# Loading FFN weight blocks a pair earlier in a hybrid decoder block, and packing float16 operands two to a buffer

## The chip, the cores and the metric

The kernel runs on one core of a Trainium2 chip. The metric is the device time of one execution in microseconds (us), lower is better. Engines are named as in the profile: PE (matrix multiply, PEld its weight loads), DVE (vector), ACT (scalar), POOL (gpsimd), SP (the queue that issues most DMAs).

## The reference

One block of a decoder on 1024 tokens of width 1024, float32. Two token mixers run side by side (dilated attention, and a gated causal convolution), they are gated and added, projected (`w_mix_out`), normalised and added to the input. A normalised SwiGLU feed-forward layer (FFN) follows:

```python
x = x + rms_norm(merged @ w_mix_out[l], g_post_mix[l])
h = rms_norm(x, g_pre_ffn[l])
x = x + rms_norm(swiglu_ffn(h, w_ffn_in[l], w_ffn_out[l]), g_post_ffn[l])

def swiglu_ffn(h, w_ffn_in, w_ffn_out):
    gate, up = jnp.split(h @ w_ffn_in, 2, axis=-1)
    return (jax.nn.silu(gate) * up) @ w_ffn_out
```

The hidden width is 2816, so `w_ffn_in` makes 22 gate blocks and 22 up blocks of 128 columns.

## The kernel before

**Precision.** Every product is made of split operands: an operand is written as a rounded part `hi` (ACT copies it) and a rest `lo` (DVE subtracts), and a product is `hi*hi + hi*lo + lo*hi`, three matmuls. In the FFN the parts are float16, and a weight block is first scaled by a power of two found from the block itself. That takes two steps. `peaks` (line 128, ACT) squares the block and sums the squares, and writes a bfloat16 column `pb` (L133 for a block, L131 for a pair). `scales` multiplies `pb` with a matrix of ones on PE (L140), which sums over the partitions, and DVE makes the scale of it (L143 to L147). Only then come the splits (L241 on ACT, L242 on DVE).

**Order by ticks.** The order on each engine is the order in which the program is written out, and each engine works strictly in that order. `tick()` is called after every few matmuls; in a tick come, in this order, the steps planned for it, one *piece* from the queue `pieces` (in each tick whose number divides by `PIECE`), and one step of each running background generator. So a piece or a planned step lands between two matmuls in PE's order, and between the work of two ticks in the order of ACT and DVE.

**Weights.** `jobs` lists all weight blocks in the order of use. `weights(i)` issues the DMA loads (L217, on SP) up to two jobs past `i`, queues the pieces of the jobs up to one past `i`, and returns the parts of block `i`; `ahead` (1 in the mixing projection) is added to both distances. A float32 block lives in a buffer of tag `b` (42 buffers of 4 KB a partition), a first block of a pair in tag `d` (3 buffers, "ring"). A plain FFN block has four pieces: `peaks`, `scales`, and a split of each half.

**Mixing projection** (L1659). Tiles of 128 tokens: first tiles 0 and 1 together, then tiles 2 to 7 one by one, each over eight blocks of `w_mix_out`. A tile has eight times six matmuls; after each six come two ticks, so a tile from 2 on has 16 ticks. `PIECE` is 2 in the first group and 3 after it. The weights of block 7 are asked for at the last of the eight blocks of the first group. After each tile a generator `mix_norm` starts: tick 1 squares (ACT L1344), tick 2 the root (L1331), ticks 3 and 4 DVE L1351, ticks 5 and 6 the addition of x (DVE L1355), tick 7 a store, tick 9 squares, root and scaled copy (ACT L1366, L1331, L1368). After tiles 3 and 7 there follow, from tick 18 on and every two ticks, four transposes on PE (L1376), a scaled copy out of them (ACT L1382) and a float16 split (L1242, L1243). PE writes `scales` and transposes into the same two PSUM banks in turn.

**FFN in.** The first two gate and two up blocks are multiplied plainly with the first and then with the second half of the tokens (`unit`: 24 matmuls, eight ticks, L368 to L372). The other 20 gate/up pairs go through `winograd`: seven products of 12 matmuls and four ticks (L384 to L386), 28 ticks a pair. Its products come in the order A11, A12, S2, S1, S3, S4, A22; S1 to S4 are sums of quarters of the two blocks. After A11 ACT copies a bank (L398), after S2 (L403; S3 goes on adding in that bank), after S1 (L408). After A12 follows DVE L1818, after S3 L1823 (A22 goes on adding in that bank), after S4 L1827. `quarters(i, c)` makes the operands of a pair in six steps: c=0 splits the first block, c=1 adds S1 and S2 (DVE L269, L270), c=2 splits them, c=3 adds S3 and S4 (L276, L277), c=4 splits them, c=5 splits A22. Steps 3 to 5 of the running pair and 0 to 2 of the next are put on ticks of the running pair by `pair`:

```python
todo = [(1, quarters(i, 3)), (8, quarters(i, 4)), (10, quarters(i, 5))]      # shortened
todo += [(LD, load_ahead(n + 1))]                                            # LD = 2
todo += [(PK, peaks(n + 1)), (SC, scales(n + 1))]                            # PK = 9, SC = 16
todo += [(k, quarters(n + 1, c)) for c, k in enumerate(PS)]                  # PS = (19, 17, 25)
```

**FFN out** (L1932) follows with its own loads and splits. `split` (L1242, L1243) makes a pair of parts in one buffer of tag `b`; for float16 it fills half of that buffer. It is used for the 16 tiles of the normalised activations (float16), the 16 activation sums T1 to T4 of the FFN (float16), and elsewhere for float32 parts.

Of the kernel before, what the change touches and what calls it, by code (L numbers as in the profile page):

```python
# [11 lines left out]
F16 = mybir.dt.float16  # L12
# [6 lines left out]
T = 1024  # L19
D = 1024  # L20
KT = 8
# [16 lines left out]

LD, PC = 2, (18, 20, 26)

PK, SC, PS = 9, 16, (19, 17, 25)

TINY, W_TOP, H_TOP = 2.0 ** -60, 2.0 ** -13, 128.0

# [21 lines left out]
def f(ap):  # L66
    return ap if ap.dtype == F16 else ap.bitcast(F32)


class Build:  # L70
# [117 lines left out]
    T, sums = None, None  # L188
# [139 lines left out]
    def timed(self, now, then, load, split):  # L328

        self.load_ahead(now[-1])  # L330
        self.queue_split(now[-1])
        self.flush(now[-1])
        self.plan.setdefault(self.ticks + load, []).append(lambda: self.load_ahead(then[-1]))
        self.plan.setdefault(self.ticks + split, []).append(lambda: self.queue_split(then[-1]))
        return [self.hl.pop(i) for i in now]

    def pair(self, i):


        J = self.jobs  # L340
        self.load_ahead(i)
        self.queue_split(i)
        self.flush(i)
        n, t = i + 1, self.ticks
        todo = [(1, lambda: self.quarters(i, 3)), (8, lambda: self.quarters(i, 4)), (10, lambda: self.quarters(i, 5))]
        if n < len(J) and J[n][2] == "row1":
            todo += [(LD, lambda: self.load_ahead(n + 1))]
            if n >= self.scaled:
                todo += [(PK, lambda: self.peaks(n + 1)), (SC, lambda: self.scales(n + 1))]
            todo += [(k, lambda c=c: self.quarters(n + 1, c)) for c, k in enumerate(PS if n >= self.scaled else PC)]  # L350
            if self.conv_sums:
                todo.append((22, self.channel_sum))
            self.queued = n + 2
        elif n < len(J):
            todo += [(3, lambda: self.load_ahead(n + 1)), (16, lambda: self.queue_split(n + 1))]
        for k, s in todo:
            self.plan.setdefault(t + k, []).append(s)
        return self.hl[i]
# [871 lines left out]
    def out_parts(self):  # L1230

        for hp in range(2):
# [3 lines left out]
            self.OT[hp] = self.both(x)  # L1236
            x = None

    def split(self, src, n, dt=F32R):
        nc = self.nc  # L1240
        s = self.slot(dt)
        nc.scalar.copy(s[:, :n], src)  # L1242
        nc.vector.tensor_tensor(s[:, 512:512 + n], src, f(s[:, :n]), op=OP.subtract)  # L1243
        return s
# [171 lines left out]
def build(ctx, tc, aps):  # L1416
    B = Build(ctx, tc, aps)
# [14 lines left out]
    glu_jobs = [(job(w_in[NG + j]), job(w_in[NU + j])) for j in range(FIRST)]  # L1432
    early = [job(w_in[NGC + n]) for n in range(8 - EARLY, 8)]
    glu_pairs = [pair(NG + j, NU + j) for j in range(FIRST, 8)]
    ga = [pair(NGA + n, NGA + n + 1) for n in range(0, 8, 2)]
    gc = [pair(NGC + n, NGC + n + 1) for n in range(0, 8 - LATE - EARLY, 2)]
    qkj = {(g, hp): pair(NK + 4 * g + hp, NQ + 4 * g + hp) for g in range(3) for hp in range(4)}
    vj = {(g, hg): (job(aps["w_v"][2 * g + hg, 0]), job(aps["w_v"][2 * g + hg, 1], kind="second"))
# [141 lines left out]
    for n, hf in [(0, 0), (1, 0), (0, 1), (1, 1)] + [(n, hf) for n in range(2, 8) for hf in range(2)]:  # L1580
# [11 lines left out]
        c = mg[n][:, hf * H:(hf + 1) * H]  # L1592
# [3 lines left out]
        if hf:  # L1596
            B.later(9, lambda n=n: nc.sync.dma_start(B.d_gc[n], mg.pop(n)))
            c = None
# [15 lines left out]
    for n in range(8):  # L1614
# [4 lines left out]
        for hf in range(2):  # L1619
            s = slice(hf * H, (hf + 1) * H)  # L1620
# [3 lines left out]
            x = B.slot(F32R)  # L1624
# [14 lines left out]
    def load_x(tt):  # L1639
        x = (B.half(), B.half())  # L1640
        for nh in range(2):
            nc.sync.dma_start(x[nh], aps["x"][tt * 128:(tt + 1) * 128, nh * H:(nh + 1) * H])
        return x
# [3 lines left out]
    for tiles in ((0, 1), (2,), (3,), (4,), (5,), (6,), (7,)):  # L1647
        banks = {tt: (B.bank(), B.bank()) for tt in tiles}
        for kt in range(KT):
            if len(W) == kt:  # L1650
                B.ahead = 1
                W.append(B.weights(mx[kt]))
            for tt in tiles:
                m = mop[tt // 4]
                o = (tt % 4) * 128
                for st, wt, a, b in ((m[kt][:, o:o + 128], W[kt][0], 1, 0), (m[kt][:, o:o + 128], W[kt][1], 0, 0),
                                     (m[kt][:, H + o:H + o + 128], W[kt][0], 0, 1)):
                    for nh in range(2):
                        nc.tensor.matmul(banks[tt][nh], st, wt[:, nh * H:(nh + 1) * H], start=bool(kt == 0 and a),  # L1659
                                         stop=bool(kt == KT - 1 and b))  # L1660
                B.tick()
                B.tick()
            if tiles[0] == 7:
                W[kt] = None
        B.PIECE = 3
        m = None
        for tt in tiles:
            if tt % 4 == 3:
                mop[tt // 4] = None
            if tt < 6:  # L1670
                xt[tt + 2] = load_x(tt + 2)
            for e in norms[:-1]:
                B.finish(e)
            norms.append(B.bg(B.mix_norm(tt, banks[tt], xt.pop(tt))))
# [2 lines left out]


    B.PIECE = 2
    held = {}  # L1680

    def spill(p, name, x):
# [129 lines left out]
    for j in range(PLAIN, FT):  # L1812
        s = [None, None]
# [108 lines left out]
    for i in range(7):  # L1922
# [12 lines left out]
        n = NP - LAST if i == 6 else NP  # L1935
        for p in range(n):
            k = i * NP + p
# [19 lines left out]
        elif i == 5:  # L1957
            for t in range(4):
                x2_load(4 + t)
                c = C[1][t][:, R]  # L1960
# [3 lines left out]
    for t in range(4):  # L1964
        for p in range(NP - LAST, NP):
            k = 6 * NP + p
# [82 lines left out]
```

## Time and profile before

| | |
|---|---|
| median of 3 runs | 1726.68 us (1723.57 to 1729.7) |
| the profiled execution, its own time | 1729.81 us |
| its span in the profile | 1728.0 us |
| PE busy | 1692.5 us (98%) |
| DVE / ACT / POOL busy | 1256.7 / 860.4 / 495.8 us |
| mean granted PE clock | 0.993 |
| mixing projection | about 991 to 1085 us of the span |
| FFN in, plain blocks | about 1085 to 1139 us |
| FFN in, 20 pairs | about 1139 to 1512 us |
| FFN out | about 1512 to 1722 us |

Times in rows are microseconds from the span's start. A row of the timeline gives start, duration, engine, line, operation, what it writes and reads, how many were merged, and in brackets how long the engine had been idle before it and which instruction ended that. A row of waits gives the total, the number and the longest. A row of windows gives the length of the stretch, the busy time and number of instructions of PE, PEld, DVE, ACT and POOL, the granted PE clock, the busy share of the DMA engines and GB/s. A matmul of 512 columns is listed with 0.38 us, but matmuls overlap, and the next starts about 0.22 us later.

### The profile page before, as it was taken

The numbers are of one execution on the slowest core, as the hardware profiler recorded it, in microseconds if no ns is written. First come the engines' busy times: TensorE is split into PE (matmuls) and PEld (weight loads), VectorE is DVE, ScalarE is ACT, GpSimd is POOL, SyncE is SP. The second block draws the span as 40 slices with busy tenths as digits, with TensorE's granted clock in tenths as the row PEclk, the third lists the DMA queues.
The fourth block names the chain that finished last, engine by engine and source line by source line (L and its number), as shares of the span: only waits on it lengthen the run. The fifth ranks groups of instructions, "written<-read, shape, count | busy, mean of one in ns | idle before, by whom it ended". The sixth has DMA issues, their size and how long they took to land.

```text
span 1728.0 us, 24733 instructions
## 1 busy us (share of the span) xinstructions
PE 1692.5 (98%) x8722; PEld 1289.3 (75%) x8722; DVE 1256.7 (73%) x2323; ACT 860.4 (50%) x1664; POOL 495.8 (29%) x386
## 2 busy tenths in 40 slices
PE   8999999999999999999999999899999999999998
PEld 7788888888888999999888887444444444488886
DVE  6789978889998656687664865586666666677586
ACT  6344343344444566667622356755445445454463
POOL 0017778887885245545300120000000000000000
PEclk9999999999999999999999999999999999999999
DMA  4352434445578697787935732212232232395244
GB/s 164 106 179 86 159 116 140 158 171 183 166 189 214 211 285 197 224 227 209 292 143 187 266 126 90 88 73 92 93 141 96 92 126 94 134 366 156 88 145 152
DMA packets 159626, 277.58 MB, mean 161 GB/s; under 512 B 47010, under 2 KB 78429, under 8 KB 159501
## 3 DMA queue, kind: packets, MB, share of 16 engines
q1 hardware_dynamic: 155292, 263.82, 47.2%
q0 software_dynamic: 3920, 11.91, 2.1%
q8 instruction: 69, 1.13, 0.3%
q14 instruction: 57, 0.46, 0.1%
q10 hardware_dynamic: 288, 0.27, 0.0%
HBM read 185.34 MB, written 95.33 MB: 162 GB/s over the span
## 4 chain that ended last, share of the span: by engine, by line
PE 82%; DMA 5%; DVE 5%; ACT 5%; issue 2%; POOL 1%; SPq 0%; DVEq 0%; ACTq 0%; POOLq 0%
PE p L384 13%; PE p L385 13%; PE p L386 13%; PE p L1932 12%; PE p L368 4%; PE p L372 4%; PE p L370 4%; PE p L1659 3%; DMA b<-w_fi 2%; PE p L1005 2%; PE p L1007 2%; PE p L1003 2%; PE p L617 2%; PE p L1101 2%; PE p L1137 1%
## 5 line engine op out<-in xcount | busy, mean ns | idle before, releaser
L384 PE MATMUL p<-b,b 128*128 128x512 f32 (+1 forms) x1124 | 432.6, 385 | 7.8 <-ACT c L403 7.8
L385 PE MATMUL p<-b,b 128*128 128x512 f32 (+1 forms) x1124 | 432.4, 385 | 0.0
L386 PE MATMUL p<-b,b 128*128 128x512 f32 (+1 forms) x1124 | 432.4, 385 | 0.0
L1932 PE MATMUL p<-b,b 128*128 128x512 f32 x924 | 209.8, 389 | 0.0
L1932 PEld LDWEIGHTS p<-b,b 128*128 128x128 f32 x924 | 173.4, 188 | 36.1
L747 DVE SCALAR_TENSOR_TENSOR p<-b,par,p 128x511 f32<-128x511 f32 (+14 forms) x232 | 163.9, 741 | 0.0
L368 PE MATMUL p<-b,b 128*128 128x512 f32 (+1 forms) x368 | 148.0, 402 | 0.0
L370 PE MATMUL p<-b,b 128*128 128x512 f32 (+1 forms) x368 | 147.1, 400 | 0.0
L372 PE MATMUL p<-b,b 128*128 128x512 f32 (+1 forms) x368 | 146.9, 399 | 0.0
L384 PEld LDWEIGHTS p<-b,b 128*128 128x128 f32 x644 | 120.9, 188 | 26.3 <-ACT c L403 0.7
L386 PEld LDWEIGHTS p<-b,b 128*128 128x128 f32 x644 | 120.9, 188 | 25.1
L385 PEld LDWEIGHTS p<-b,b 128*128 128x128 f32 x644 | 120.9, 188 | 24.9
L251 POOL TENSOR_TENSOR b<-d,b 128x1024 fp32r<-128x1024 f32 x44 | 106.9, 2429 | 79.9 <-ACT b L250 72.4
L1003 PE MATMUL p<-b,b 128*128 128x256 f32 x384 | 116.0, 302 | 0.0
L1005 PE MATMUL p<-b,b 128*128 128x256 f32 x384 | 115.2, 300 | 0.0
L1007 PE MATMUL p<-b,b 128*128 128x256 f32 x384 | 115.1, 300 | 0.0
L1242 ACT CAST b<-b 128x512 fp32r<-128x512 f32 (+1 forms) x117 | 72.2, 619 | 46.6 <-PE p L1932 18.0
L1243 DVE TENSOR_TENSOR b<-c,b 128x512 fp32r<-128x512 f32 (+1 forms) x101 | 70.4, 698 | 33.2 <-ACT b L1242 32.9
L385 PEld LDWEIGHTS <-b 128*128 128x128 f16 x480 | 46.9, 98 | 62.6 <-issue 8.2
L1243 DVE TENSOR_TENSOR b<-b,b 128x512 fp32r<-128x512 f32 (+1 forms) x117 | 80.1, 689 | 17.9 <-ACT b L1242 16.1
L1659 PE MATMUL p<-b,b 128*128 128x512 f32 x384 | 89.7, 392 | 0.0
L384 PEld LDWEIGHTS <-b 128*128 128x128 f16 x480 | 47.0, 98 | 56.9 <-issue 0.4
(273 smaller groups left out, 3530.4 us busy)
## 6 DMA issues: line engine op xcount, KB each, us to landing
b<-w_in SPq DMA_DIRECT2D x30, 512.0 KB, 4.7
dk<-c SPq DMA_DIRECT2D x48, 256.0 KB, 2.8
dq<-c SPq DMA_DIRECT2D x48, 256.0 KB, 3.7
b<-dq SPq DMA_DIRECT2D x48, 256.0 KB, 8.6
b<-dk SPq DMA_DIRECT2D x48, 256.0 KB, 7.0
b<-w_fi SPq DMA_DIRECT2D x24, 512.0 KB, 4.8
d<-w_in SPq DMA_DIRECT2D x23, 512.0 KB, 3.7
dqS<-c SPq DMA_DIRECT2D x44, 256.0 KB, 2.1
```

The source lines that it names most:

```text
L368: nc.tensor.matmul(ps, hi[:, s], a, start=kt == 0, stop=False)
L370: nc.tensor.matmul(ps, hi[:, s], b, start=False, stop=False)
L372: nc.tensor.matmul(ps, lo[:, s], a, start=False, stop=kt == nk - 1)
L384: nc.tensor.matmul(ps, hi[:, s], a, start=first and kt == 0, stop=False, skip_group_check=True)
L385: nc.tensor.matmul(ps, hi[:, s], b, start=False, stop=False, skip_group_check=True)
L386: nc.tensor.matmul(ps, lo[:, s], a, start=False, stop=kt == 3, skip_group_check=True)
L747: nc.vector.scalar_tensor_tensor(A[i][:, j:], src[i][:, :H - j], w[i], A[i][:, j:], op0=OP.mult, op1=OP.add)
L1003: nc.tensor.matmul(o, a, hi[:, s], start=kt == 0, stop=False)
L1005: nc.tensor.matmul(o, a, lo[:, s], start=False, stop=False)
L1007: nc.tensor.matmul(o, b, hi[:, s], start=False, stop=kt == KT - 1)
L1243: nc.vector.tensor_tensor(s[:, 512:512 + n], src, f(s[:, :n]), op=OP.subtract)
L1932: nc.tensor.matmul(acc[t], x, y, start=first and e == 0, stop=last and e == 2, skip_group_check=True)
```

## The change

- `weights(mx[7])`, at the last block of the first group of the mixing projection, looks 3 jobs further instead of 1. So all four plain FFN blocks get their pieces queued there (before: two), and the loads go on to the first pair.
- In the FFN `ahead` is 0 from the start of the plain blocks (before: 1 for them, then 0).
- In `pair`, `peaks` of the next pair moves from tick 9 to tick 5, `scales` from 16 to 12, and the steps 0, 1 and 2 of its `quarters` from ticks 19, 17, 25 to 18, 20, 26. A new step at tick 20 loads the pair after the next; the load at tick 2 finds its pair loaded.
- `split` to float16 takes half of a shared buffer: two consecutive calls share one (`packed`).

```diff
-PK, SC, PS = 9, 16, (19, 17, 25)
+LF, PK, SC = 20, 5, 12
...
             if n >= self.scaled:
+                todo += [(LF, lambda: self.load_ahead(n + 3))]
                 todo += [(PK, lambda: self.peaks(n + 1)), (SC, lambda: self.scales(n + 1))]
-            todo += [(k, lambda c=c: self.quarters(n + 1, c)) for c, k in enumerate(PS if n >= self.scaled else PC)]
+            todo += [(k, lambda c=c: self.quarters(n + 1, c)) for c, k in enumerate(PC)]
...
+    spare = None
+
+    def packed(self):
+        if self.spare is None:
+            x = self.slot(F16, [128, 2 * T])
+            self.spare = x[:, T:]
+            return x[:, :T]
+        x, self.spare = self.spare, None
+        return x
+
     def split(self, src, n, dt=F32R):
         nc = self.nc
-        s = self.slot(dt)
+        s = self.packed() if dt == F16 else self.slot(dt)
...
             if len(W) == kt:
-                B.ahead = 1
+                B.ahead = 1 if kt < KT - 1 else 3
                 W.append(B.weights(mx[kt]))
...
     B.PIECE = 2
+    B.ahead = 0
     held = {}
```

`PC` is (18, 20, 26), as before.

## The prediction

> **What bounds the kernel now.** First the busy times: PE is the bound nearly everywhere, so only its own waits and its slow clock can be won back.
>
> ```profile
> span 1728.0 us, 24733 instructions
> PE 1692.5 (98%) x8722; PEld 1289.3 (75%) x8722; DVE 1256.7 (73%) x2323; ACT 860.4 (50%) x1664; POOL 495.8 (29%) x386
> ```
>
> Next, who made PE wait. These rows are of the whole span, save the last two, which are of the stretch 1155 to 1512 us (the pairs of the FFN).
>
> ```profile
> PE p L384 <- ACT c L403: 7.8, 11, 0.9
> PE p L140 <- ACT pb L133: 6.1, 1, 6.1
> PE p L1376 <- ACT b L1368: 1.7, 1, 1.7
> PE p L1376 <- ACT b L1382: 0.5, 2, 0.4
> PE p L384 <- DVE c L1823: 0.7, 1, 0.7
> ...
> PE p L384 <- ACT c L403: 6.7, 9, 0.9
> ACT junk L128 <- DMA d<-w_fi: 32.0, 18, 2.4
> ```
>
> The change touches all of them. Then the two places in order of time. The 6.1 us wait lies in the plain FFN blocks:
>
> ```profile
> 1089.36 1.33 ACT L241 ACTIVATE b<-b,sc 128x512 f16<-128x512 f32 x2 [2.10 <-DVE sc L146]
> ...
> 1092.59 1.05 ACT L1366 ACTIVATE b<-d 128x1024 f32<-128x1024 f32 x1
> ...
> 1093.75 1.28 ACT L1331 ACT_TABLE_LOAD   x1
> ...
> 1096.20 1.15 ACT L1368 ACTIVATE b<-d,rr 128x1024 f32<-128x1024 f32 x1 [0.87 <-DVE rr L1336]
> 1097.26 1.04 ACT L128 ACTIVATE junk<-b 128x1024 bf16<-128x1024 f32 x1
> ...
> 1098.42 0.19 ACT L133 CAST pb<-pk 128x1 bf16<-128x1 f32 x1
> ...
> 1098.66 0.16 PE L140 MATMUL p<-pb,ones 128*128 128x1 bf16 x1 [6.13 <-ACT pb L133]
> ```
>
> `peaks` of the fourth FFN block stands on ACT behind the last tile's normalisation (L1366 to L1368), and `scales` stands in PE's order in front of matmuls that have all they need. The pattern to remember: a piece is placed by ticks, that is by PE's progress; if ACT is late, PE waits at L140. In the pairs ACT is late by the weight's DMA instead:
>
> ```profile
> 1255.08 0.41 SPq L217 DMA_DIRECT2D d<-w_fi  x1
> 1258.85 1.06 ACT L128 ACTIVATE junk<-d 128x1024 bf16<-128x1024 f32 x1 [1.82 <-DMA d<-w_fi]
> 1260.18 1.06 ACT L128 ACTIVATE junk<-b 128x1024 bf16<-128x1024 f32 x1 [0.18 <-DMA b<-w_fi]
> 1262.18 0.56 ACT L403 COPY c<-p 128x512 f32<-128x512 f32 x1
> 1262.79 0.38 PE L384 MATMUL p<-b,b 128*128 128x512 f16 x1 [0.62 <-ACT c L403]
> ```
>
> **The change, part by part.**
>
> *Pairs.* The load now stands at tick 20 of the pair before. SP gets to it behind the same stores as today, so some 4 us into that pair, and 3.8 us later (1255.08 to 1258.85) it has landed, more than 10 us before `peaks` asks. The two squares with their column (1262.18 less 0.7 for an L241, less 1258.85, less the waits: 2.4 to 2.8 us) run at tick 5, right after L398. What may be late next is L1823, since S1 and S2 are now added after the first block's split. An undisturbed pair:
>
> ```profile
> 1273.35 0.58 ACT L398 COPY c<-p 128x512 f32<-128x512 f32 x1 [3.73 <-PE p L386]
> 1281.15 0.57 ACT L408 COPY c<-p 128x512 f32<-128x512 f32 x1
> 1281.73 1.15 ACT L241 ACTIVATE b<-d,sc 128x1024 f16<-128x1024 f32 x1
> 1281.73 0.68 DVE L269 TENSOR_TENSOR d<-b 128x512 f32<-128x512 f32 x1
> 1282.45 0.69 DVE L270 TENSOR_TENSOR d<-d,d 128x512 f32<-128x512 f32 x1
> 1283.06 1.28 DVE L242 SCALAR_TENSOR_TENSOR b<-d,sc,b 128x1024 f16<-128x1024 f32 x1
> 1284.26 0.68 DVE L1823 TENSOR_TENSOR c<-p,c 128x512 f32<-128x512 f32 x1
> 1286.12 0.38 PE L384 MATMUL p<-b,c 128*128 128x512 f16 x1
> 1288.71 0.38 PE L384 MATMUL p<-b,b 128*128 128x512 f16 x1
> ```
>
> Twelve matmuls take 1288.71 - 1286.12 = 2.59 us, so this pair began at 1286.12 - 6 x 2.59 = 1270.6, and A22 starts at 15.55. L398 comes 0.2 us after its product's end (1273.35 against 1270.6 + 2.6), at 2.8. Behind it run the squares (2.8), the split of S3 and S4 (1.15) and that of A22 (0.7): ACT is free at 8.0, just when L403 is due (3 x 2.59 + 0.2), and PE wants that bank only at 10.4. So the 6.7 us go. L408 can come at 4 x 2.59 + 0.2 = 10.6. From there: L241 11.1 to 12.2, L242 12.3 to 13.5, L269 and L270 to 14.9, L1823 to 15.5. That is 0.05 us before A22 wants the bank. I take 0 for it; the ends are 0 and 0.04 x 20 = 0.8 us. In the first pair, where DVE is also making T3 and T4, no such room exists: L1823 was late there already (0.7 us above). The two adds in front of it are 1.4 us, which bounds the loss; the gain is bounded by 0. I take 0.7.
>
> *Plain blocks.* With four blocks prepared, no L140 stands in the first two units. The wait goes (6.13 us idle, and 0.16 more since the next matmul normally starts 0.16 before the listed end of the last: 6.3), and the slow clock behind it:
>
> ```profile
> 632.50:639.20 6.70, 6.70 (x34) 6.70 (x33) 2.38 (x9) 2.33 (x7) 0.00 (x0) 0.50 1.04 246
> 833.90:840.60 6.70, 6.70 (x26) 5.94 (x26) 4.12 (x14) 4.87 (x15) 1.51 (x2) 0.50 0.55 177
> 1096.70:1103.40 6.70, 4.74 (x13) 1.70 (x13) 2.02 (x6) 5.70 (x11) 0.00 (x0) 0.50 0.07 30
> ```
>
> The granted clock is 0.50 in each of these, and PE was busy 4.74 us of the third: 2.4 us lost. Together 8.7 us. A part comes back: the first pair's squares (2.8 us of ACT) ran inside the wait; now they run just before the transposes.
>
> ```profile
> 1105.56 0.69 ACT L1382 ACTIVATE b<-p,gain 128x512 f32<-128x512 f32 x1 [2.23 <-PE p L1376]
> ...
> 1117.91 0.38 PE L368 MATMUL p<-b,b 128*128 128x512 f16 x1
> ```
>
> Here ACT had been idle for 2.23 us, so L1382 came right behind the first transposes. Prompt again, it would come 8.7 us earlier, at 1096.9. L1366 today stands behind the third block's splits (to 1090.69), a table load (1.28, like the one shown) and an activation; without the splits the load is over before the first unit ends, and the chain comes up to 2.0 us earlier: L1368 ends at 1095.4, before the transposes need it. Then the squares end near 1098.1, so L1382 is 1.2 us late, and with two PSUM banks PE waits by my count 0.1 at L140 and 0.6 and 0.2 at transposes, where it waited 0.1 (the smaller of the two waits for L1382). The fifth unit, at 1117.91 now, starts at 1110.0: a gain of 7.9 us. The ends are 8.7 and, with the waits at three of the eight transposes instead of two and as long as the first, 6.5.
>
> *Mixing projection.* The four pieces of the third block and four of the fourth now run here, with `PIECE` 3. Where do they fall?
>
> ```profile
> 990.90:1023.93 33.03, 32.94 (x144) 26.96 (x145) 1.00 0.38 140
> ...
> 1015.63 0.18 PE L140 MATMUL p<-pb,ones 128*128 128x1 bf16 x1
> ...
> 1024.00:1034.00 10.00, 10.00 (x46) 8.29 (x45) 4.84 (x18) 7.13 (x14) 0.00 (x0) 1.00 0.46 159
> ...
> 1030.34 1.15 ACT L1368 ACTIVATE b<-d,rr 128x1024 f32<-128x1024 f32 x1 [0.87 <-DVE rr L1336]
> 1031.40 0.70 ACT L241 ACTIVATE b<-b,sc 128x512 f16<-128x512 f32 x1
> ```
>
> The first row, a window of this line alone, counts the matmuls of L1659: 96 of the first group and 48 of tile 2, which ends at 1023.93. The L140 inside it stands after two sixes of tile 2, at tick 4; it is `scales` of the second block. Its splits follow at ticks 7 and 10, so `peaks` of the third block falls on tick 13 and its `scales` on tick 16: in PE's order directly before tile 3. In ACT's order that `peaks` stands behind the split of tick 10, the L241 of 1031.40, which itself stands behind tick 9, where two tiles' normalisations end at 1031.5. So ACT comes to it at 1032.1, 8 us after PE has left tile 2. The square and its column add 1.05 + 0.19 + 0.19 (less overlaps of 0.1): `pb` is there at 1033.4, and PE, which arrives at 1023.9, waits 9.5 us. It is the wait of 1092 in another place, and longer. Behind it stands a slow clock: by the third row 2.4 us at least; by two slow stretches joined, the second wholly busy, 0.9 + 3.4 = 4.3. I take 3.4, one full busy stretch, as in the first two rows.
>
> By the rule of the Trainium skill ("TensorE: Matmul & The Clock Gate", Part 1), a PE that idled through a window runs its first 3.4 us at half rate; as an estimate that is 1.7 us lost, and the sum below would be 1721.9. The traced stretches disagree: 6.7 us long with PE wholly busy.
>
> PE, then 13 us late, finds ACT ready at the first transposes: 1.7 plus 0.4 us of waits go; I take 2.1 (1.7 to 2.1). `scales` of the fourth block (tile 3, tick 12) comes 8 us after the wait and its `peaks` 4 us after: no wait. The added squares and splits (1.4 + 1.4 us of ACT a block) run beside matmuls there; ACT has 2.9 of 10 us free even in the second row's stretch. If that cover were gone, 5.6 us of ACT would lie on the path.
>
> *Packing and loads.* The parts' sizes and operations stay; 8 buffers come free, which the earlier raw and scaled blocks use. `d` has three buffers, one now held from here on; a tile's normalisation then reuses the buffer of the last tile but one, whose store is two tiles old. Cost 0; if that cover were gone, a store of some microseconds would delay ACT, not PE.
>
> *Sum.* -6.7 (pairs) + 0.7 (first pair) - 7.9 (plain blocks) + 9.5 + 3.4 - 2.1 (mixing) = -3.1 us. The profiled execution took 1729.81 (span 1728.0), so it would take 1726.7; its own time stands 3.1 us above the median of the runs shown, 1726.68, from which I forecast 1723.6. With all ends one way: -8.7 - 6.7 + 9.5 + 2.4 - 2.1 = -5.6 (1721.1), and -6.5 - 5.9 + 1.4 + 9.5 + 4.3 - 1.7 = +1.1 (1727.8). A measurement of this kernel tells about 0.3% (5.2 us) from no change.
>
> **Rivals.**
> 1. *No wait at tile 3* (ACT gets there in time). For it: ACT is only 71% busy between 1024 and 1034 (7.13 of 10). Against: it works in order, and its row at 1030.34 waits for DVE, not PE. Without 9.5 and 3.4: 1723.6 - 12.9 = 1710.7.
> 2. *Slower: L1823 behind the two adds holds A22 in every pair.* The room is 0.05 us; if L408 or the split come late, every pair pays. It decides from 0.41 us a pair (20 x 0.41 = 8.3, from -3.1 to +5.2); at 0.45 the time is 1732.6. Against: every step above has its duration from a row, and in the pair shown L269 and L270 already ran before L1823; only L242 and they change places.
> 3. *The loads do nothing*: `peaks` at tick 5 makes ACT late for L403 by itself, and the 6.7 us stay: 1730.3. Against: 2 us of room.
>
> **How the numbers follow.** My forecast has 0.70, rival 1 0.12, rival 2 0.10, rival 3 0.08. The forecast's own range is 1721 to 1728, and with the scatter of the runs a third of it lies more than 0.3% below: 0.23. Faster 0.23 + 0.12 = 0.35; within 0.3% 0.45 + 0.04 = 0.49; slower 0.02 + 0.10 + 0.04 = 0.16. The range takes in the forecast, rival 3 and the near end of rival 2: 1715 to 1732.
>
> **What would show it.** Right: no wait at L140 in the plain blocks; a new wait of PE at L140 for L133 of 9 to 10 us near 1024, with a stretch at clock 0.50 behind it; no wait of L384 for L403 in the pairs, and ACT L128 no longer waiting for DMA; L1823 ending close to A22's start. Wrong: no such wait near 1024 (rival 1), or rows of L384 waiting for L1823 in many pairs (rival 2).

## The result and the profile after

| | before | after |
|---|---|---|
| median of 12 runs each, us | 1727.3 (1723.21 to 1732.61) | 1721.53 (1717.23 to 1726.85) |
| ratio, 95% interval | | 0.9967 (0.9954 to 0.998) |
| the profiled execution: its time, its span | 1729.81, 1728.0 | 1718.91, 1717.1 |

The changed kernel is 5.8 us faster by the medians, 0.33%. Lines past 348 move by 1 in the new file, past 1240 by 11 or 12: L384 is now L385, L403 L404, L1366 L1377, L1368 L1379, L1376 L1387, L1382 L1393, L1659 L1670, L1823 L1835; L128, L140, L241 and L269 keep their numbers. In the kernels of the experiments the later lines lie a few lines elsewhere again (L1835 of the changed kernel is L1840 in one and L1844 in another).

Who made PE wait, over the whole span of the changed kernel (total us, times, longest; the waits of the stages ahead of the mixing projection left out):

```profile
PE p L140 <- ACT pb L133: 9.4, 1, 9.4
...
PE p L385 <- DVE c L1835: 2.4, 1, 2.4
PE p L1387 <- ACT b L1393: 0.4, 2, 0.2
...
PE p L1387 <- DVE sc L143: 0.3, 1, 0.3
PE p L385 <- ACT c L404: 0.2, 1, 0.2
```

The total for L403 has fallen from 7.8 to 0.2. The wait at L140 has not gone: it has grown from 6.1 to 9.4 and changed its place. (The 2.4 us for L1835, which was L1823 with 0.7, lie in the first pair.) The timeline shows where the wait at L140 is now:

```profile
1025.59 1.15 ACT L1379 ACTIVATE b<-d,rr 128x1024 f32<-128x1024 f32 x1 [0.87 <-DVE rr L1347]
1026.65 0.70 ACT L241 ACTIVATE b<-b,sc 128x512 f16<-128x512 f32 x1
1027.26 1.04 ACT L128 ACTIVATE junk<-b 128x1024 bf16<-128x1024 f32 x1
1028.21 0.19 ACT L128 ACTIVATION_READ_ACCUMULATOR junk<-b 128x1 f32 x1
1028.42 0.19 ACT L133 CAST pb<-pk 128x1 bf16<-128x1 f32 x1
...
1028.67 0.16 PE L140 MATMUL p<-pb,ones 128*128 128x1 bf16 x1 [9.35 <-ACT pb L133]
```

The normalisation of tile 1 (L1379), the second block's split (L241), and only then the third block's square and its `pb`: the order that the prediction read off the ticks.

The rows of stages, first before, then after: the mixing projection to tile 2, tiles 3 to 5, the first four plain units, pairs 1 and 2, pairs 3 to 20. Tiles 6 and 7 (21.9 us) and the last four plain units (20.7 us) take the same in both and are left out. (Columns: stretch, length, busy time and instructions of PE, PEld, DVE, ACT, POOL, PE clock, DMA share, GB/s.)

```profile
991.00:1023.94 32.94, 32.94 (x147) 26.91 (x146) 21.98 (x50) 16.23 (x34) 9.57 (x6) 1.00 0.38 140
1023.94:1062.69 38.75, 36.72 (x178) 29.99 (x176) 21.21 (x66) 24.96 (x49) 0.00 (x0) 1.00 0.37 123
...
1084.56:1117.91 33.35, 27.07 (x132) 13.74 (x132) 16.89 (x42) 26.51 (x44) 0.00 (x0) 0.90 0.18 66
...
1138.63:1176.74 38.11, 36.62 (x172) 16.55 (x171) 29.55 (x48) 21.11 (x32) 0.00 (x0) 1.00 0.23 84
1176.74:1511.58 334.84, 327.98 (x1530) 148.92 (x1529) 218.23 (x341) 169.25 (x253) 0.00 (x0) 1.00 0.31 112
```

```profile
986.21:1028.69 42.48, 33.13 (x148) 26.84 (x147) 26.37 (x63) 23.27 (x47) 9.58 (x6) 0.93 0.49 185
1028.69:1067.52 38.83, 38.62 (x178) 31.42 (x178) 20.75 (x63) 23.68 (x47) 0.00 (x0) 0.95 0.24 82
...
1089.40:1114.50 25.10, 24.67 (x130) 13.09 (x130) 13.15 (x30) 21.37 (x34) 0.00 (x0) 1.00 0.20 73
...
1135.22:1174.08 38.86, 36.47 (x172) 16.43 (x170) 29.62 (x48) 21.11 (x32) 0.00 (x0) 1.00 0.31 109
1174.08:1500.66 326.58, 326.58 (x1531) 148.25 (x1529) 217.19 (x341) 170.81 (x253) 0.00 (x0) 1.00 0.31 112
```

| stage | before | after | difference |
|---|---|---|---|
| mixing, to tile 2 | 32.94 | 42.48 | +9.5 |
| mixing, tiles 3 to 5 | 38.75 | 38.83 | +0.1 |
| first four plain units | 33.35 | 25.10 | -8.2 |
| pairs 1 and 2 | 38.11 | 38.86 | +0.8 |
| pairs 3 to 20 | 334.84 | 326.58 | -8.3 |
| sum of these | | | -6.1 |

The sum stands beside the -5.8 of the medians. The spans differ by 10.9; the other 4.8 lie before 986 us, where no instruction was changed (a single profile of each). So stages are compared below, and whole times only by the runs.

### The profile page after: what moved, and what is told of

Its sections match the earlier page's. It is cut to its first block, busy times and chain, and to the rows that moved or that the text cites. A ratio compares the mean times of both kernels' runs of the same rounds, so it can differ in the third digit from the quotient of the medians.

```text
span 1717.1 us, 24763 instructions
## 1 busy us (share of the span) xinstructions
PE 1686.3 (98%) x8722; PEld 1285.2 (75%) x8722; DVE 1255.3 (73%) x2323; ACT 861.7 (50%) x1664; POOL 495.8 (29%) x386
## 4 chain that ended last, share of the span: by engine, by line
PE 90%; DMA 3%; ACT 3%; DVE 2%; issue 1%; POOL 1%; DVEq 0%; SPq 0%; ACTq 0%; POOLq 0%
PE p L385 15%; PE p L386 15%; PE p L387 15%; PE p L1944 12%; PE p L369 5%; PE p L373 4%; PE p L371 4%; PE p L1670 4%; PE p L1006 2%; PE p L1004 2%; PE p L1008 2%; PE p L618 2%; PE p L1102 2%; PE p L1138 1%; DMA c<-rep 1%; PE p L1161 1%
## 5 line engine op out<-in xcount | busy, mean ns | idle before, releaser
L385 PE MATMUL p<-b,b 128*128 128x512 f32 (+1 forms) x1124 | 432.6, 385 | 0.2 <-ACT c L404 0.2
L1944 PEld LDWEIGHTS p<-b,b 128*128 128x128 f32 x924 | 173.5, 188 | 36.1
L385 PEld LDWEIGHTS p<-b,b 128*128 128x128 f32 x644 | 120.9, 188 | 26.3 <-ACT c L404 0.7
L387 PEld LDWEIGHTS p<-b,b 128*128 128x128 f32 x644 | 120.9, 188 | 25.1
L386 PEld LDWEIGHTS p<-b,b 128*128 128x128 f32 x644 | 120.9, 188 | 25.0
L1670 PE MATMUL p<-b,b 128*128 128x512 f32 x384 | 92.0, 398 | 0.0
L1670 PEld LDWEIGHTS p<-b,b 128*128 128x128 f32 x384 | 72.6, 192 | 24.2 <-DVE b L242 9.4
L385 PEld LDWEIGHTS <-b 128*128 128x128 f16 x480 | 46.9, 98 | 56.7
```

What stands on the lines that cost most here:

```text
L385: nc.tensor.matmul(ps, hi[:, s], a, start=first and kt == 0, stop=False, skip_group_check=True)
L386: nc.tensor.matmul(ps, hi[:, s], b, start=False, stop=False, skip_group_check=True)
L387: nc.tensor.matmul(ps, lo[:, s], a, start=False, stop=kt == 3, skip_group_check=True)
L1944: nc.tensor.matmul(acc[t], x, y, start=first and e == 0, stop=last and e == 2, skip_group_check=True)
```

## The experiments

Each kernel was timed several times, against several runs of the kernel before on the same chip. The stage times, in us, are of one profile of each kernel.

| kernel | ratio to before (95%) | mixing to t2 | t3 to 5 | units 1-4 | pairs 1-2 | pairs 3-20 |
|---|---|---|---|---|---|---|
| before | 1 | 32.9 | 38.8 | 33.4 | 38.1 | 334.9 |
| the change | 0.9967 (0.9954 to 0.998) | 42.5 | 38.8 | 25.1 | 38.9 | 326.6 |
| pairs only | 0.9952 (0.9936 to 0.9967) | 33.0 | 38.8 | 33.5 | 38.8 | 326.6 |
| plain blocks only | 1.0007 (0.9996 to 1.0017) | 42.5 | 39.3 | 25.1 | 38.1 | 335.9 |
| packing only | 1.0003 (0.9992 to 1.0014) | 33.0 | 38.8 | 33.0 | 38.1 | 335.9 |
| loads only | 0.9949 (0.9932 to 0.9966) | 33.0 | 38.8 | 32.4 | 38.1 | 326.6 |
| adds first | 0.9951 (0.9934 to 0.9968) | 42.5 | 39.3 | 25.1 | 38.2 | 326.6 |
| squares early | 0.9937 (0.9918 to 0.9955) | 33.1 | 44.7 | 25.1 | 38.9 | 326.6 |
| squares early, splits late | 0.9915 (0.9894 to 0.9936) | 33.0 | 38.7 | 25.1 | 40.5 | 326.6 |
| the same with adds first | 0.9893 (0.9875 to 0.9911) | 33.0 | 38.7 | 25.1 | 38.2 | 326.6 |

The theory is that of the prediction: three waits of PE, each behind ACT, one in the pairs removed, one in the plain blocks removed, one new before tile 3. The rivals: that the gain comes from preparing the plain blocks, or from freed buffers, or from the new ticks and not the loads.

**Pairs only.** The mixing projection and the plain blocks are as before; the packing stays. The edit is shown against the changed kernel.

```diff
-                B.ahead = 1 if kt < KT - 1 else 3
+                B.ahead = 1
...
     B.PIECE = 2
-    B.ahead = 0
     held = {}
```

> Only the pairs are changed (loads a pair ahead, squares at tick 5, adds at tick 20, float16 parts two to a buffer); the mixing projection and the plain blocks are as before. Theory (three waits of PE, one removed in the pairs, one in the plain blocks, one new at tile 3): no wait near tile 3, the 6.1 us wait at L140 in the plain blocks is back, the pairs from the third on take 326.6 us instead of 334.9, the first two 0.8 us more than before. That is 7.5 us below the kernel before (ratio 0.9957), so 1 to 2 us faster than the whole change. Rival (the earlier loads in the mixing projection bring the gain): no faster than before, ratio 1.000.

Measured: 0.9952, 1720.58 us. The waits of PE from 980 to 1520 us:

```profile
PE p L140 <- ACT pb L133: 6.1, 1, 6.1
PE p L385 <- DVE c L1834: 2.3, 1, 2.3
PE p L1387 <- ACT b L1379: 1.7, 1, 1.7
PE p L1387 <- ACT b L1393: 0.4, 1, 0.4
```

The old wait of 6.1 is back, the new one gone, the pairs keep their gain. The whole gain of the change is there (0.9952 against 0.9967).

**Plain blocks only.** The change without its edits in `pair` (constants and `todo` as before).

> Only the plain blocks are changed (four prepared in the mixing projection, float16 parts two to a buffer); the pairs are as before. Theory: 9.5 us wait at L140 before tile 3 and 2 to 3.4 us of slow clock there, 1.9 to 2.1 us of waits at the transposes gone, 8.2 us gone in the first four plain units. Sum 9.5 + 2.0 to 3.4 - 2.0 - 8.2 = +1.3 to +2.7 us against before (ratio 1.0008 to 1.0016): no gain. Rival (the gain comes from here): 5 us below before, ratio 0.997.

Measured: 1.0007. This half of the change gives nothing: 8.2 us gained in the plain units, 9.5 lost before tile 3, and the transposes' waits traded for the slow clock (the stretch at a granted PE clock of 0.50 behind the new wait). By its stages it is 2.9 us slower than before, a little over the expected 1.3 to 2.7; 1.1 of them lie in the pairs, which this half does not touch.

**Packing only.** The kernel before, with `packed` in `split`.

> The kernel before with the float16 parts two to a buffer and nothing else. Theory: the parts' sizes and operations stay, no instruction waited for a buffer on the path: ratio 1.000 within 0.0015, the waits of PE as before (6.1 at L140, 6.7 at L403 in the pairs). Rival (freed buffers let work start earlier): 2 us or more below before.

Measured: 1.0003; the wait at L140 is 6.1, that at L403 8.0 us. Freed buffers alone bring nothing. The pairs from the third on took 335.9 us in both profiles that have the packing and the old pairs, 1.1 more than before, with 7.3 and 7.6 us of waits at L403 there instead of 6.7; whether that is the packing or scatter of single profiles stays open. (The plain half of the change holds more blocks in the mixing projection; it was not tried without packing.)

**Loads only.** The kernel before with one step more in `pair`.

```diff
-PK, SC, PS = 9, 16, (19, 17, 25)
+LF, PK, SC, PS = 20, 9, 16, (19, 17, 25)
...
             if n >= self.scaled:
+                todo += [(LF, lambda: self.load_ahead(n + 3))]
                 todo += [(PK, lambda: self.peaks(n + 1)), (SC, lambda: self.scales(n + 1))]
```

> The kernel before with the loads of the pairs at tick 20 of the pair before, and nothing else: squares stay at tick 9, scales at 16, adds at 17. Theory (ACT is late because the squares wait for the DMA): the waits of L384 for L403 go (8.3 us of the pairs from the third on), the first pair stays as it was, ratio 0.9952. Rival (squares in front of L403 are the cause, wherever their data is): the waits stay, and moving the squares to tick 5 is what helped: ratio 1.000.

Measured: 0.9949, 1719.87 us. The squares stay at tick 9, and the nine waits at L403 in the pairs from the third on are gone all the same (the first pair keeps its own, 0.8 us). What ACT waited for in the pairs, first before (1177 to 1511 us), then here (1177 to 1503):

```profile
ACT junk L128 <- DMA d<-w_fi: 30.9, 17, 2.4
...
ACT junk L128 <- DMA b<-w_fi: 2.3, 12, 0.3
```

```profile
ACT c L1831 <- DVE c L1828: 49.6, 18, 3.2
ACT c L399 <- DMA dqS<-c: 33.6, 9, 3.7
ACT c L399 <- PE p L387: 33.6, 9, 3.7
ACT c L409 <- PE p L140: 19.4, 17, 1.4
...
ACT c L404 <- PE p L387: 6.1, 9, 3.0
...
```

L128 stands nowhere in the second list, and ACT, early now, waits for PE at L404 nine times instead of once. The cause in the pairs was the DMA, not the place of the squares. The new ticks bring nothing: pairs 3 to 20 take 326.58 us with and without them, and pairs 1 and 2 take 38.10 here against 38.86.

**Adds first.** The change, with the steps of the next pair back on ticks 19, 17, 25 (adds ahead of the first block's split).

> The whole change, but with the steps 0, 1, 2 of the next pair at ticks 19, 17, 25 as before: DVE makes the two adds (L269, L270) before the split of the first block. Theory (the 2.4 us wait of the first pair is L1823 behind these adds): that wait falls to 0.7 us or less, the other pairs do not change: 1.7 us below the changed kernel, ratio to the kernel before 0.9957. Rival (DVE's work on T3 and T4 makes L1823 late whatever the order): the wait stays at 2.4 us, ratio 0.9967.

Measured: 0.9951, pairs 1 and 2 at 38.22. The interval of the ratio (0.9934 to 0.9968) holds what either side expected, so the stage has to decide, and it agrees with neither: the wait for L1835 falls from 2.4 to 1.7, not to 0.7, and does not stay. The order mattered for 0.64 us of the two pairs; the rest is DVE's own work. From the changed kernel's first pair, DVE's last rows and, after them, the row of ACT that they hang on:

```profile
1148.83 0.69 DVE L1714 TENSOR_TENSOR c<-c,c 128x512 f32<-128x512 f32 x1
1150.07 1.28 DVE L242 SCALAR_TENSOR_TENSOR b<-d,sc,b 128x1024 f16<-128x1024 f32 x1 [0.55 <-issue]
...
1152.60 0.68 DVE L1835 TENSOR_TENSOR c<-p,c 128x512 f32<-128x512 f32 x1
```

```profile
1148.83 1.15 ACT L241 ACTIVATE b<-d,sc 128x1024 f16<-128x1024 f32 x1 [1.25 <-DVE sc L146]
```

DVE has a pause of 0.55 us ahead of its part of the first block's split (L242). The row names no releaser for it, but the split's other part on ACT (L241) ends at 1149.98 and L242 begins at 1150.07.

With the adds first that pause is filled, and DVE works from 8.6 us to 17.4 us of that pair without a listed gap. The expectation of 0.7 took over the old wait for L1823 without the old wait for L403 (0.8) ahead of it: in the kernel before both together held PE 1.5 us, and DVE ended at the same place of the pair (17.3).

**Squares early.** The change, but the squares of the third and fourth block are written out as soon as they are loaded; in the changed kernel ACT is idle there from 996.7 to 1006.1, waiting for a first scale:

```profile
1006.06 1.34 ACT L241 ACTIVATE b<-b,sc 128x512 f16<-128x512 f32 x2 [9.32 <-DVE sc L146]
```

```diff
-                self.pieces.append((j, lambda j=j: self.peaks(j)))
+                if j not in self.peak:
+                    self.pieces.append((j, lambda j=j: self.peaks(j)))
...
                 B.ahead = 1 if kt < KT - 1 else 3
+                if kt == KT - 1:
+                    B.load_ahead(fi[1][1])
+                    for i in fi[1]:
+                        B.peaks(i)
                 W.append(B.weights(mx[kt]))
```

> The whole change, but the squares of the third and fourth FFN block come on ACT as soon as they are loaded, at the last block of the first group of the mixing projection, ahead of the normalisations of tiles 0 and 1; scales and splits stay pieces. Theory (the wait before tile 3 is the square standing behind these normalisations): no wait at L140, 9.5 + 2.0 us go. But then PE is no longer late for the first transposes: their 2.1 us of waits come back, and up to 2.9 us more, since four splits (0.7 us each) now stand before them on ACT. So 6.5 to 9.4 us below the changed kernel, ratio to before 0.991 to 0.993. Rival (the wait is for something else, a load or a buffer): the wait stays, ratio 0.9967.

Measured: 0.9937. No wait at L140. The waits of PE between 1025 and 1080 us:

```profile
PE p L1388 <- ACT b L1380: 5.1, 1, 5.1
PE p L1388 <- ACT b L1394: 0.2, 1, 0.2
```

This shows the cause of the wait before tile 3. The other half of the expectation came true in kind, and larger: with PE on time, ACT is late for the first transposes by 5.1 us (expected 2.1 to 5.0), and a slow clock of 6.8 us, which the expectation did not have, begins in that wait. So the stages are only 3.6 us below the changed kernel, not 6.5 to 9.4, and the ratio lies just outside the expected 0.991 to 0.993, though its interval (0.9918 to 0.9955) reaches into that. Not only the splits stand ahead of the transposes. ACT also waits for the scale of the fourth block, which DVE makes behind additions of a normalisation:

```profile
1041.13 0.72 ACT L241 ACTIVATE b<-b,sc 128x512 f16<-128x512 f32 x1 [3.35 <-DVE sc L146]
```

**Squares early, splits late.** Instead of pieces, `scales` and the two splits of both blocks are planned on ticks 2 to 17 after the start of tile 6.

```diff
-                B.ahead = 1 if kt < KT - 1 else 3
+                B.ahead = 1
+                if kt == KT - 1:
+                    B.load_ahead(fi[2][1])
+                    for i in fi[1]:
+                        B.peaks(i)
+                    for e, i in enumerate(fi[1]):
+                        for n, s in enumerate((lambda i=i: B.scales(i), lambda i=i: B.part(i, 0), lambda i=i: B.part(i, 1))):
+                            B.later(4 + 66 + 9 * e + 3 * n, s)
                 W.append(B.weights(mx[kt]))
+                if kt == KT - 1:
+                    B.queued = fi[1][1] + 1
```

> As with the early squares, but scales and splits of the third and fourth FFN block are planned on ticks of tiles 6 and 7, behind the transposes. Theory: no wait at L140, and at the transposes the 2.1 us of before and no more: 9.4 us below the changed kernel, ratio to before 0.991. Rival (ACT has no room there either): new waits of the same size in tile 7 or in the plain blocks.

Measured: 0.9915, 1713.74 us against the expected 0.991. Mixing is back at 33.0 and 38.7 us, the plain units stay at 25.1; tiles 6 and 7 take 22.2 instead of 21.9. Pairs 1 and 2 show 40.5, because in this profile the 2.3 us wait for DVE was followed by a slow clock:

```profile
1148.30:1151.60 3.30, 3.30 (x9) 1.18 (x8) 1.91 (x2) 0.70 (x1) 0.00 (x0) 0.50 0.13 52
```

**Both repairs.** The same with the adds first.

> Early squares, late scales and splits, and the adds first in the pairs (ticks 19, 17, 25). Theory: the two repairs add up: 9.4 + 1.7 us below the changed kernel, 16 to 17 us below the kernel before, ratio 0.990.

Measured: 0.9893 (0.9875 to 0.9911), 1710.83 us, 18.6 us below the runs of the kernel before beside it. It beats both kernels. Its waits from 980 to 1520 us:

```profile
PE p L385 <- DVE c L1844: 1.7, 1, 1.7
PE p L1387 <- ACT b L1379: 1.6, 1, 1.6
PE p L1387 <- ACT b L1393: 0.5, 2, 0.4
PE p L1387 <- DVE sc L143: 0.3, 1, 0.3
```

Expected was 0.990. Its stages give -16.2 us against before, a ratio of 0.9906, inside the interval.

## Why the prediction was right, and where its sizes were off

The forecast was 3.1 us faster, 5.8 were measured. The time, 1721.53 us, lies near the lower edge of the forecast's own range (1721 to 1728). The largest of its chances, 0.49, was on a change within 0.3%; the measured 0.33%, with an interval of 0.20 to 0.46, does not decide between that and a little more. The steps held, each in its place. Two terms were mis-sized, those of the pairs and of the slow clock, and one was right by two errors that cancel, that of the first pair.

- *Pairs* (-6.7): measured -8.3, and shown to be the DMA's by the kernel with the loads alone. The mechanism was right, the size read wrongly: a listed wait starts at the listed end of a matmul, 0.16 us after the next would have started. The prediction added this to the wait in the plain blocks and forgot it for the nine waits here: 6.7 + 9 x 0.16 = 8.1.
- *L1823 in the pairs* (0): right. ACT and DVE ran the pair on the predicted schedule: L409 (L408 before) at 10.6 us of the pair, L1835 ending at 15.5, about 0.1 us before A22. Rival 2 did not come about, by that margin.

```profile
1275.44 0.58 ACT L409 COPY c<-p 128x512 f32<-128x512 f32 x1 [0.94 <-PE p L387]
1277.10 1.29 DVE L242 SCALAR_TENSOR_TENSOR b<-d,sc,b 128x1024 f16<-128x1024 f32 x1 [2.12 <-ACT b L241]
1279.63 0.68 DVE L1835 TENSOR_TENSOR c<-p,c 128x512 f32<-128x512 f32 x1
...
1280.42 0.38 PE L385 MATMUL p<-b,c 128*128 128x512 f16 x1
```

(The pair's first matmul starts at 1264.85; the last row is A22's first.)

- *First pair* (+0.7): +0.8 for the first two, and that is luck. The wait for L1835 (L1823 before) grew from 0.7 to 2.4 us, by 1.7, which is more than the bound of 1.4. But the wait for L403 that stood ahead of it there (0.8 us) went, and the sum had not counted that one.
- *Plain blocks* (-7.9): -8.2.
- *Wait before tile 3* (9.5): the stage grew by 9.5. Rival 1 fell with it, and the early squares showed the cause.
- *Slow clock behind it* (3.4): 2.0. The clock fell 3.1 us into the listed wait (which began at 1019.32) and rose 4.0 us after it:

```profile
1022.42:1028.68 6.26, 0.01 (x1) 0.01 (x1) 1.61 (x6) 5.33 (x10) 0.00 (x0) 0.50 0.41 134
1028.68:1032.65 3.97, 3.97 (x10) 3.17 (x10) 3.22 (x13) 3.85 (x10) 0.00 (x0) 0.50 0.00 0
1032.66:1040.00 7.34, 7.34 (x34) 5.89 (x33) 3.60 (x13) 2.90 (x5) 0.00 (x0) 1.00 0.44 145
```

The prediction took a whole busy stretch of 6.7 us, as in two rows of the trace before; the stretch here was 10.2 us, but 6.3 of it lay inside the wait. The estimate by the Trainium skill ("TensorE: Matmul & The Clock Gate", Part 1), 1.7 us, was the nearer one in this profile. In those of plain blocks only and adds first, which have the same wait, the clock rose 5.05 and 4.92 us after it; that is 2.5 us lost, about midway between 1.7 and 3.4, and it is why their tiles 3 to 5 take 39.3 us. In the upper end of this term (0.9 + 3.4) the 0.9 does not come out of the prediction's row at 1096.70: there the clock fell 4.2 us into the wait, which would leave 0.7.
- *Transposes* (-2.1): tiles 3 to 5 grew by 0.1 with 2.0 us of slow clock in them, so -1.9.

The wrongly read pairs (1.6) and the clock (1.4) make up the 3.0 us between -3.1 and the -6.1 of the stages; the differences in the other terms (-0.3, +0.1, +0.2) cancel.

## What to carry to other kernels

Where work is placed in an engine's order by the progress of another engine, look up how far the two are apart at that place before moving anything there: the same square and scale cost nothing in one place, 6.1 us in a second and 9.5 in a third. Put the slow producer's step early and its consumer late, each on its own schedule; a fixed distance of three ticks holds only while both engines keep step. And try the parts of a change alone: one line here (the load) carried the whole gain; another part gave nothing, and some 8 us (of the -16.2, what lies outside the pairs) once the new wait that came with it was removed.

## What the runs showed of the hardware that was not expected

- The PE clock can fall for much shorter waits than 9 us: after the 2.3 us wait for DVE in the first pair a stretch at 0.50 followed (the row at 1148.30). In the profiles of three other kernels (the change, pairs only, squares early) a wait of 2.3 or 2.4 us at the same place had none; pairs 1 and 2 ran at clock 1.00. So the same wait cost a further 1.6 us (40.49 against 38.86 for pairs 1 and 2) or nothing. What decides was not tested.
- Between the first and the last microseconds of the program every stretch at clock 0.50 in these ten profiles lasted 3.4, 6.8 or 10.2 us. Worked out as half of the time in it that PE is busy, what such a stretch costs depends on how much of it lies inside the wait: 10.2 us cost 2.0 in the changed kernel, 6.8 cost 2.4 in the kernel before. The stages fit: tiles 3 to 5 take 38.8 us with 2.0 and 39.3 with 2.5.
- These stretches are a part of the scatter of the runs: the stage ahead of the mixing projection, the same instructions in all kernels, took 986.2 us with 3.4 us at clock 0.50 in one profile (the change) and 992.5 with 13.7 in another (squares early).
